# Scores and value products of both row tiles issued as one group in every attention

## The chip, the cores and the metric

One NeuronCore of a Trainium2 chip runs the kernel. The metric is the device time of one execution in microseconds (us). The engines are named as the profile names them: PE is TensorE (PEld its weight loads), DVE is VectorE, ACT is ScalarE, POOL is GpSimd, SP the engine that issues the DMAs.

## The reference, cut to what matters

Two decoder layers over 256 positions of width 1024, all in float32. Each layer projects the normed input and runs four causal mixers of 4 heads x 64; one of them, NSA, has three parts, of which two are ordinary attentions here. So a layer has five attentions of the same form (DSA with a mask of selected keys, MoBA, two of NSA, and SWA with a sink and a band of 128):

```
h = rms_norm(x, norm1_g[l]);  proj = h @ w_in[l]
ya = dsa_mixer(...); yb = moba_mixer(...); yc = nsa_mixer(...); yd = swa_mixer(...)
br = einsum('bsnc,ncd->bsnd', [ya, yb, yc, yd], w_branch[l])
x = x + einsum('bsnd,bsnd->bsd', sigmoid(g_br), br) @ w_out[l]
x = x + conv_ffn(rms_norm(x, norm2_g[l]), ...)

each attention:  s = q k^T * scale;  p = masked_softmax(s, ok, sink);  o = p v
NSA:             g0 * o_compressed + g1 * o_selected + g2 * o_window
```

## The kernel before, in words

The 256 positions are two row tiles of 128 (`NT` = 2); row tile t sees 128 (t + 1) keys. Every large product takes its float32 operands as a rounded high part and a low part (`hi`, `lo`; fp32r), three matmuls for each. ACT makes the high part of the weights and DVE the low part, in pieces of 128 x 1024, just ahead of their use.

The order on each engine is written by a planner in the kernel itself (`Flow`, line 86). Every part of the work is a Python generator, a stream. It asks for an engine, the times that it needs and the buffers that it wants (`yield "PE", needs, rings`), and then issues instructions. `Flow.run` (line 139) goes on each time with the stream that can start first by its own estimate of durations (`Eng.cost`, line 180); of equal starts the lower priority number goes first. A request for several buffers waits until all are free. The chip then runs each engine's instructions in that fixed order.

`main` (line 1261) is the stream that fills PE. For each layer it issues the projections, then gates, hidden products and branches in the order of `SEQ` (line 398): gate 0 twice, hidden 0 and 1, gate 1 twice, branch 0 and 1 (two halves each), gate 2 twice, branch 2 (two halves), gate 3, branch 3, gate 3, branch 3. A gate takes 48 matmuls of 512 columns into two banks. A branch half takes 12 and needs the finished result `yf` of its mixer, split by `y_T` (line 587). `hidden` (line 1039) needs `hid.ready`, from the first part of `nsa`.

There are eight PSUM banks in three rings: `mm_r` with four, `sc_r` with two, `tr_r` with two (lines 252 to 254). `main` takes its banks from `mm_r`, two at a time (first branch halves from `sc_r` once all mixers are done).

`attend(t, ...)` (line 642) is one attention for one row tile; each attention spawns two such streams, with neighbouring priorities. It takes a softmax buffer `sx_r` (a ring of two), small columns `sm_r` (four) and both banks of `sc_r`. Its scores are four matmuls on row halves of the array (64 rows contract; even and odd heads lie in the two halves and write different banks). Then `attend_max` (line 747) reads the banks on DVE with scale, mask and running maximum; after that come exponentials on ACT, the reciprocal, the scaling, transposes of the probabilities on PE through `tr_r`, their copy into a buffer of `pt_r` (a ring of two), and the value products on column halves of the array (64 output rows each). The result is copied, or for NSA added, into `y`. In the trace a score matmul is `sc<-qk` with 64*128 in front, a value product `tr<-f,slotQ` or `tr<-f,kvA` with 128*64; a float32 matmul leaves two records, so a score group has 8 records, and a value group has 8 for row tile 0 and 16 for row tile 1.

`nsa` needs its compressed part `y0` before its two attentions begin. The hidden products also use small tiles (128*15).

## Time and profile before

| | us |
|---|---|
| median of three runs (849.93 to 850.3) | 850.2 |
| the profiled execution | 850.6 |
| its span, first to last instruction | 848.8 |
| PE busy | 839.5 (99%) |
| DVE busy | 668.4 (79%) |
| ACT busy | 549.6 (65%) |

A view of the timeline gives start and duration in us, the engine, the line (every instruction is recorded at the helper's line 215), the operation, what it writes and reads, and its shape; "x8" is a run of eight instructions merged into one row, and in brackets stands idle time of the engine in front of it. PE's matmuls are pipelined, so a duration is longer than the distance between starts; it is the starts that give the pace.

### The profile page before, as it was taken

How to read it: one execution, taken by the hardware profiler on the slowest of the kernel's cores; microseconds unless marked ns; L12 is line 12 of the kernel's file. 1: busy time of each engine (PE TensorE's matmuls, PEld its weight loads, DVE VectorE, ACT ScalarE, POOL GpSimd, SP SyncE). 2: the span in 40 equal slices, each digit the busy share in tenths (PEclk: the TensorE clock that was granted, in tenths of full speed). 3: DMA queues.
4: the chain of work that ended last, by engine and by line, in shares of the span. 5: the costliest groups of instructions: out<-in, count | busy, mean ns of one | idle time of the engine just before them, and what ended most of it. 6: DMA issues, size and time to landing. Idle time of an engine off the chain costs nothing.

```text
span 848.8 us, 14195 instructions
## 1 busy us (share of the span) xinstructions
PE 839.5 (99%) x5457; PEld 730.2 (86%) x5457; DVE 668.4 (79%) x1310; ACT 549.6 (65%) x968; POOL 34.2 (4%) x33
## 2 busy tenths in 40 slices
PE   9999999999999999999999999999999999999998
PEld 8987777778889999988899877777788999999886
DVE  5899897867669999985457998898856799999552
ACT  6664965664558888864356568567645788888431
POOL 0011111000000000000001010110000000000000
PEclk9999999999999999999999999999999999999999
DMA  7754444525646665546445564544365465556550
GB/s 264 248 199 149 147 164 150 182 80 203 217 151 205 212 206 196 188 151 219 146 131 179 195 198 158 191 149 143 110 200 193 149 199 198 200 198 199 176 196 26
DMA packets 103415, 149.92 MB, mean 177 GB/s; under 512 B 4072, under 2 KB 62258, under 8 KB 103346
## 3 DMA queue, kind: packets, MB, share of 16 engines
q1 hardware_dynamic: 103346, 149.00, 52.5%
q8 instruction: 43, 0.70, 0.4%
q14 instruction: 26, 0.21, 0.1%
HBM read 147.94 MB, written 1.05 MB: 176 GB/s over the span
## 4 chain that ended last, share of the span: by engine, by line
PE 85%; DVE 8%; DMA 3%; ACT 2%; issue 1%; POOL 0%; SPq 0%; DVEq 0%; ACTq 0%
PE mm L215 74%; PE tr L215 6%; PE sc L215 5%; DVE lo L215 2%; DMA raw<-in_w_in_dram 2%; DVE acc L215 2%; DVE m L215 1%; ACT f L215 1%; DVE f L215 1%; DMA x<-in_x_dram 1%; ACT hi L215 1%; DVE rt L215 0%; SPq L243 0%; POOL rkC L215 0%; DVE kr L215 0%
## 5 line engine op out<-in xcount | busy, mean ns | idle before, releaser
L215 DVE TENSOR_TENSOR lo<-raw,hi 128x1024 fp32r<-128x1024 f32 (+2 forms) x280 | 328.4, 1177 | 103.2 <-ACT hi L215 99.2
L215 ACT ACTIVATE hi<-raw 128x1024 fp32r<-128x1024 f32 (+2 forms) x280 | 283.5, 1022 | 147.8 <-PE mm L215 131.0
L215 PE MATMUL mm<-hi,ahi 128*128 128x512 f32 (+4 forms) x480 | 176.2, 373 | 0.6 <-ACT hi L215 0.6
L215 PE MATMUL mm<-hi,alo 128*128 128x512 f32 (+4 forms) x480 | 171.9, 364 | 0.4 <-DVE alo L215 0.4
L215 PE MATMUL mm<-ahi,hi 128*128 128x256 f32 x640 | 149.8, 276 | 0.0
L215 PE MATMUL mm<-alo,hi 128*128 128x256 f32 x640 | 149.6, 276 | 0.0
L215 PEld LDWEIGHTS mm<-alo,hi 128*128 128x128 f32 x640 | 120.2, 188 | 0.1
L215 PEld LDWEIGHTS mm<-ahi,hi 128*128 128x128 f32 x640 | 120.1, 188 | 0.1
L215 PE MATMUL mm<-lo,ahi 128*128 128x512 f32 (+4 forms) x480 | 119.0, 371 | 0.0
L215 PEld LDWEIGHTS mm<-hi,ahi 128*128 128x128 f32 x480 | 90.2, 188 | 14.1 <-issue 1.1
L215 PEld LDWEIGHTS mm<-hi,alo 128*128 128x128 f32 x480 | 90.4, 188 | 12.6 <-DVE alo L215 0.7
L215 PEld LDWEIGHTS mm<-lo,ahi 128*128 128x128 f32 x480 | 82.6, 188 | 14.6 <-issue 2.9
L215 PE MATMUL mm<-hi,slotQ 128*128 128x512 f32 x352 | 89.7, 395 | 0.0
L215 PE MATMUL mm<-ahi,lo 128*128 128x256 f32 x640 | 86.9, 276 | 0.0
L215 PEld LDWEIGHTS mm<-hi,slotQ 128*128 128x128 f32 x352 | 66.1, 188 | 15.5
L215 PEld LDWEIGHTS mm<-ahi,lo 128*128 128x128 f32 x640 | 79.1, 188 | 0.0
L215 ACT ACTIVATE f<-f,col 128x256 f32<-128x256 f32 x88 | 48.1, 594 | 6.3 <-DVE f L215 5.8
L215 PE MATMUL mm<-lo,slotQ 128*128 128x512 f32 x176 | 48.7, 396 | 0.0
L215 ACT ACTIVATE f<-f,nmx 128x128 f32<-128x128 f32 (+1 forms) x80 | 35.5, 446 | 13.1 <-DVE nmx L215 13.1
L215 PEld LDWEIGHTS mm<-lo,slotQ 128*128 128x128 f32 x176 | 33.0, 188 | 7.7
L215 ACT ACTIVATE qk<-f,col 128x256 f32<-128x256 f32 x88 | 39.2, 495 | 0.0
L215 DVE SCALAR_TENSOR_TENSOR f<-f,col,f 128x254 f32<-128x254 f32 x88 | 38.2, 477 | 0.0
(229 smaller groups left out, 1037.8 us busy)
## 6 DMA issues: line engine op xcount, KB each, us to landing
raw<-in_w_up_dram SPq DMA_DIRECT2D x44, 1024.0 KB, 5.1
raw<-in_w_in_dram SPq DMA_DIRECT2D x40, 1024.0 KB, 4.9
raw<-in_w_down_dram SPq DMA_DIRECT2D x20, 1024.0 KB, 4.9
raw<-in_w_out_dram SPq DMA_DIRECT2D x8, 1024.0 KB, 4.9
raw<-in_w_branch_dram SPq DMA_DIRECT2D x6, 1024.0 KB, 4.8
raw<-in_w_in_dram SPq DMA_DIRECT2D x7, 768.0 KB
raw<-in_w_in_dram SPq DMA_DIRECT2D x4, 592.0 KB, 3.7
raw<-in_w_in_dram SPq DMA_DIRECT2D x4, 536.0 KB, 5.6
```

The costliest lines, as they stand in the source:

```text
L215: fn(*a, **k)
```

## The change

`attend` is replaced by three streams. `attend2` asks once for two softmax buffers, two sets of small columns, two banks of `mm_r` (row tile 0) and two of `sc_r` (row tile 1), and issues the scores of both row tiles, eight matmuls, in one group. `softmax` runs once for each row tile with what stood between scores and value products, and `values` waits for all transposed probabilities of both row tiles, issues the 12 value matmuls in one group into one bank of `tr_r`, and makes one copy or addition of the whole `y`. `SEQ` and `main` stay as they are. The planner's cost of a matmul changes as well: it charged 95 when the type of operand changed between fp32 and fp32r, and now charges 100 when the tile shape (`side`) does.

```diff
@@ -175,7 +175,7 @@
 
     def __init__(self, flow, name, real):
         self.flow, self.name, self.real = flow, name, real
-        self.side, self.rounded = 1, True
+        self.side, self.tiled = 1, 1
 
     def cost(self, m, a, k):
         aps = [v for v in list(a) + list(k.values()) if hasattr(v, "shape")]
@@ -186,10 +186,9 @@
             if m == "transpose":
                 c = 0.835 * n
             else:
-                r = a[1].dtype == F32R
-                c = 0.446 * n + 2 if r else 1.67 * max(n, free_size(a[1])) + 2
-                if r != self.rounded:
-                    c, self.rounded = c + 95 * self.side, r
+                c = 0.446 * n + 2 if a[1].dtype == F32R else 1.67 * max(n, free_size(a[1])) + 2
+                if self.side != self.tiled:
+                    c, self.tiled = c + 100 * self.side, self.side
             return c / self.side * (1 if self.flow.clock["PE"] > 6700 else 2)
         ptrs = sum(hasattr(k.get(q), "shape") for q in ("scale", "bias", "accum_out", "scalar"))
         if self.name == "ACT":
@@ -639,23 +638,56 @@
         tr_r.give(tb, te)
         return te
 
-    def attend(t, qT, kblk, kT, vfn, scl, mask, y, needs, sink=None, fin=None, gate=None):
+    def attend2(prio, qT, kblk, kT, vfn, scl, masks, y, needs, sink=None, fin=None, gates=None):
+
+        got = yield "PE", needs, [sx_r, sm_r, sx_r, sm_r, mm_r, mm_r, sc_r, sc_r]
+        P.side = 2
+        for t in range(NT):
+            nk = 128 * (t + 1)
+
+            for hh in range(2):
+                for par in range(2):
+                    b = 64 * par
+                    te = P.matmul(got[4 + 2 * t + par][:, hh * nk:hh * nk + nk], qT[b:b + 64, hh, t * 128:t * 128 + 128],
+                                  kT[b:b + 64, kblk(2 * hh + par), :nk], start=True, stop=True)
+        P.side = 1
+        pts, evs = [None, None], [[Fut() for _ in range(t + 1)] for t in range(NT)]
+        for t in range(NT):
+            fl.spawn(softmax(t, got[2 * t], got[2 * t + 1], got[4 + 2 * t:6 + 2 * t], (mm_r, sc_r)[t], te, scl, masks[t], sink,
+                             None if gates is None else gates[t], pts, evs[t]), prio + t)
+        yield from values(vfn, pts, evs, y, gates is not None, fin)
+
+    def values(vfn, pts, evs, y, more, fin):
+
+        ob, = yield "PE", evs[0] + evs[1], [tr_r]
+        op = ob.rearrange("p (k q) -> p k q", k=2)
+        P.side = 2
+        for t in range(NT):
+            pT = pts[t].rearrange("p (h b q) -> p h b q", h=H, b=2)
+            for k in range(2):
+                for b in range(t + 1):
+                    for par in range(2):
+                        te = P.matmul(op[64 * par:64 * par + 64, k, t * 128:t * 128 + 128], vfn(2 * k + par, b),
+                                      pT[:, 2 * k + par, b, :], start=b == 0, stop=b == t)
+            pt_r.give(pts[t], te)
+        P.side = 1
+        if not more:
+            eng, _ = yield "AV", [te], []
+            te = copy_on(eng, y, op)
+        else:
+            yield "DVE", [te], []
+            te = V.tensor_tensor(y, y, op, op=ALU.add)
+        tr_r.give(ob, te)
+        fin(te)
+
+    def softmax(t, sxt, sm, scs, ring_, te, scl, mask, sink, gate, pts, tes):
         nk = 128 * (t + 1)
         rdf = Fut()
         tx = []
-        sxt, sm, *scs = yield "PE", needs, [sx_r, sm_r, sc_r, sc_r]
         Sx = sxt.rearrange("p (h n) -> p h n", h=H)
         mx, nmx, den, es, rd = (sm[k] for k in ("mx", "nmx", "den", "es", "rd"))
-
-        P.side = 2
-        for hh in range(2):
-            for par in range(2):
-                b = 64 * par
-                te = P.matmul(scs[par][:, hh * nk:hh * nk + nk], qT[b:b + 64, hh, t * 128:t * 128 + 128],
-                              kT[b:b + 64, kblk(2 * hh + par), :nk], start=True, stop=True)
-        P.side = 1
         for par in range(2):
-            fl.spawn(attend_max(t, scs[par], te, par, Sx, nk, mask, scl, sink, mx, tx), 8)
+            fl.spawn(attend_max(t, scs[par], te, par, Sx, nk, mask, scl, sink, mx, tx, ring_), 8)
         yield "DVE", [_Pair(tx)], []
         tm = V.tensor_scalar(nmx, mx, -1.0, None, op0=ALU.mult)
         for h in range(H):
@@ -678,11 +710,10 @@
                 tn.append(A.activation(Sx[:, h, :nk], Sx[:, h, :nk], AF.Copy, scale=rd[:, h:h + 1]))
             else:
                 tn.append(V.tensor_scalar(Sx[:, h, :nk], Sx[:, h, :nk], rd[:, h:h + 1], None, op0=ALU.mult))
-        tes = []
-        pTt = None
         for g in range(t + 1):
             if g == 0:
                 pTt, tb = yield "PE", tn if t == 0 else tn[:2], [pt_r, tr_r]
+                pts[t] = pTt
                 pT = pTt.rearrange("p (h b q) -> p h b q", h=H, b=2)
             else:
                 tb, = yield "PE", tn[2:], [tr_r]
@@ -697,31 +728,9 @@
                     for b in range(2):
                         tq = P.transpose(tp[:, hh, b, :], Sx[:, 2 * g + hh, b * 128:b * 128 + 128], ident)
                 dst = pT[:, 2 * g:2 * g + 2]
-            f = Fut()
-            tes.append(f)
-            fl.spawn(evac_tr(dst, tp, tb, tq, f), 9)
+            fl.spawn(evac_tr(dst, tp, tb, tq, tes[g]), 9)
         sx_r.give(sxt, tq)
         sm_r.give(sm, max(tn))
-
-        ob, = yield "PE", tes, [tr_r]
-        op = ob[:, :256].rearrange("p (k q) -> p k q", k=2)
-        P.side = 2
-        for k in range(2):
-            for b in range(t + 1):
-                for par in range(2):
-                    te = P.matmul(op[64 * par:64 * par + 64, k, :], vfn(2 * k + par, b), pT[:, 2 * k + par, b, :],
-                                  start=b == 0, stop=b == t)
-        P.side = 1
-        pt_r.give(pTt, te)
-        yt = y[:, :, t * 128:t * 128 + 128]
-        if gate is None:
-            eng, _ = yield "AV", [te], []
-            te = copy_on(eng, yt, op)
-        else:
-            yield "DVE", [te], []
-            te = V.tensor_tensor(yt, yt, op, op=ALU.add)
-        tr_r.give(ob, te)
-        fin(te)
 
     def recip(t2, den, rd, gate, f):
         yield "DVE", [t2], []
@@ -744,14 +753,14 @@
         def t(self):
             return max(self.l) if len(self.l) == 2 else None
 
-    def attend_max(t, sc, te, par, Sx, nk, mask, scl, sink, mx, tx):
+    def attend_max(t, sc, te, par, Sx, nk, mask, scl, sink, mx, tx, ring_):
         for hh in range(2):
             h = 2 * hh + par
             yield "DVE", [te], []
             td = V.tensor_tensor_reduce(Sx[:, h, :nk], sc[:, hh * nk:hh * nk + nk], mask, scale=scl[:, t, h:h + 1],
                                         scalar=LOW if sink is None else sink[:, h:h + 1],
                                         op0=ALU.add, op1=ALU.max, accum_out=mx[:, h:h + 1])
-        sc_r.give(sc, td)
+        ring_.give(sc, td)
         tx.append(td)
 
     def evac_tr(dst, tp, tb, te, f):
@@ -844,10 +853,9 @@
         tq = yield from T_pairs(qT, qr, 2, [tq])
         tk = yield from T_pairs(kT, krd, 1, [tk])
         prep_r.give(prep, tk)
-        fin = qk_done(qk, [], yf, NT)
-        for t in range(NT):
-            fl.spawn(attend(t, qT, lambda h: 0, kT, lambda h, b: kvA[:, b, 64:128], th(sm1["sA"], H), sel[t],
-                            y, [tq, tk, self_f[t]], fin=fin), 10 + t)
+        fin = qk_done(qk, [], yf, 1)
+        fl.spawn(attend2(10, qT, lambda h: 0, kT, lambda h, b: kvA[:, b, 64:128], th(sm1["sA"], H), sel,
+                        y, [tq, tk] + self_f, fin=fin), 10)
 
     def indexer(t, iqT, ikT, iw, needs, fin, f):
         nk = 128 * (t + 1)
@@ -901,10 +909,9 @@
         tk = yield from rope(kr.rearrange("p t (h u d) -> p t h u d", u=1, d=64), heads(kn), H, DH, cc[:, 3], ss_[:, 3], rt, [tn])
         tk = yield from T_pairs(kT, kr, 2, [tk])
         prep_r.give(prep, tk)
-        fin = qk_done(qk, [], yf, NT)
-        for t in range(NT):
-            fl.spawn(attend(t, qT, lambda h: h // 2, kT, lambda h, b: pb[:, b, 512 + 64 * h:576 + 64 * h],
-                            th(sm1["sB"], H), tri[:, 128 * (1 - t):], y, [tq, tk], fin=fin), 20 + t)
+        fin = qk_done(qk, [], yf, 1)
+        fl.spawn(attend2(20, qT, lambda h: h // 2, kT, lambda h, b: pb[:, b, 512 + 64 * h:576 + 64 * h],
+                        th(sm1["sB"], H), [tri[:, 128:], tri], y, [tq, tk], fin=fin), 20)
 
     def swa(l, pd, pf, y, yf):
         (prep,) = yield "ACT", [pf, tab_f[l]], [prep_r]
@@ -923,11 +930,10 @@
         tk = yield from rope(kr.rearrange("p t (h u d) -> p t h u d", h=2, d=64), knv, 2, DH, cc[:, 9], ss_[:, 9], rt, [tn], dup=2)
         tk = yield from T_pairs(kT, kr, 2, [tk])
         prep_r.give(prep, tk)
-        fin = qk_done(qk, [], yf, NT)
-        for t in range(NT):
-            fl.spawn(attend(t, qT, lambda h: h // 2, kT,
-                            lambda h, b: pd[:, b, 384 + 64 * (h // 2):448 + 64 * (h // 2)], th(sm1["sD"], H),
-                            tri[:, 128:] if t == 0 else dmask, y, [tq, tk], sink=M[l]["sink"], fin=fin), 30 + t)
+        fin = qk_done(qk, [], yf, 1)
+        fl.spawn(attend2(30, qT, lambda h: h // 2, kT,
+                        lambda h, b: pd[:, b, 384 + 64 * (h // 2):448 + 64 * (h // 2)], th(sm1["sD"], H),
+                        [tri[:, 128:], dmask], y, [tq, tk], sink=M[l]["sink"], fin=fin), 30)
 
     def nsa(l, pc, pf, y, yf, hid):
         m = M[l]
@@ -1010,7 +1016,7 @@
         tr_r.give(tb, te)
         y0 = [Fut(), Fut()]
         fl.spawn(nsa_cmp(qT, [te, tq], tvb, cgv, y, y0), 12)
-        fin = qk_done(qk, [], yf, 2 * NT)
+        fin = qk_done(qk, [], yf, 2)
         last = list(y0)
         for i, g in ((0, 6), (1, 7)):
             off = 384 + 128 * i
@@ -1025,10 +1031,9 @@
             tk = yield from T_pairs(kTi, krd, 1, [tk])
             if i == 1:
                 prep_r.give(prep, tk)
-            for t in range(NT):
-                fl.spawn(attend(t, qT, lambda h: 0, kTi, lambda h, b, off=off: pc[:, b, off + 64:off + 128],
-                                th(sm1["sC"], H), tri[:, 128 * (1 - t):], y, [tq, tk, y0[t]],
-                                fin=fin, gate=cgv[:, t, :, 1 + i]), 13 + 2 * i + t)
+            fl.spawn(attend2(13 + 2 * i, qT, lambda h: 0, kTi, lambda h, b, off=off: pc[:, b, off + 64:off + 128],
+                             th(sm1["sC"], H), [tri[:, 128:], tri], y, [tq, tk, y0[0]],
+                             fin=fin, gates=[cgv[:, t, :, 1 + i] for t in range(NT)]), 13 + 2 * i)
 
     class Hidden:
 
```

## Rows read from the trace of the kernel before

**Rows 1.** The page: busy us, share of the span and instructions of each engine.

```profile
PE 839.5 (99%) x5457; PEld 730.2 (86%) x5457; DVE 668.4 (79%) x1310; ACT 549.6 (65%) x968; POOL 34.2 (4%) x33
```

**Rows 2.** Windows: stretch, its us, busy us of each engine (instructions), PEclk, DMA share, GB/s.

```profile
56.00:109.50 53.50, 52.56 (x319) 40.75 (x317) 51.28 (x161) 39.26 (x87) 5.17 (x2) 1.00 0.42 138
109.50:187.20 77.70, 76.44 (x478) 59.49 (x477) 62.57 (x175) 47.77 (x114) 6.03 (x3) 1.00 0.45 156
...
451.00:610.00 159.00, 157.99 (x989) 126.75 (x989) 140.11 (x391) 107.52 (x229) 12.96 (x8) 1.00 0.48 163
```

**Rows 3.** Timeline of PE around a score group of row tile 0.

```profile
89.09 0.40 PE L215 MATMUL mm<-hi,alo 128*128 128x512 f32 x1
89.42 0.72 PE L215 MATMUL sc<-qk 64*128 64x128 f32 x8
90.06 0.50 PE L215 MATMUL mm<-hi,ahi 128*128 128x512 f32 x1
90.40 0.39 PE L215 MATMUL mm<-hi,alo 128*128 128x512 f32 x1
```

**Rows 4.** Timeline of PE, a value group directly followed by a score group, row tile 1.

```profile
95.31 0.40 PE L215 MATMUL mm<-hi,alo 128*128 128x512 f32 x1
95.64 1.09 PE L215 MATMUL tr<-f,kvA 128*64 128x128 f32 x16
96.66 1.14 PE L215 MATMUL sc<-qk 64*128 64x256 f32 x8
97.72 0.74 PE L215 MATMUL mm<-lo,ahi 128*128 128x512 f32 x2
```

**Rows 5.** Timeline of PE, a full-size fp32 group and matmuls behind it.

```profile
33.38 0.61 PE L215 MATMUL tr<-kvup,kn 128*128 128x128 f32 x4
...
33.95 0.29 PE L215 MATMUL mm<-hi,alo 128*128 128x268 f32 x1
34.07 0.29 PE L215 MATMUL mm<-hi,ahi 128*128 128x268 f32 x1
```

**Rows 6.** Timeline of PE, last gate matmuls and the hidden products, layer 0.

```profile
102.54 0.86 PE L215 MATMUL mm<-lo,ahi 128*128 128x512 f32 x3
...
109.53 1.94 PE L215 MATMUL mm<-raw,kr 128*15 128x128 f32 x64
```

**Rows 7.** Timeline of DVE: merge, first mask-and-max step, and the split behind the fourth.

```profile
146.23 1.28 DVE L215 SCALAR_TENSOR_TENSOR mg<-mg,mm 128x512 f32<-128x512 f32 x2
147.43 0.34 DVE L215 CUSTOM_DVE_ANT_0 f<-sc,cst,sC 128x128 f32<-128x128 f32 x1
...
148.51 1.22 DVE L215 TENSOR_TENSOR lo<-raw,hi 128x1024 fp32r<-128x1024 f32 x1
```

**Rows 8.** Timeline of PE, score groups of NSA, and last that of SWA.

```profile
146.35 0.71 PE L215 MATMUL sc<-qk 64*128 64x128 f32 x8
...
165.02 0.71 PE L215 MATMUL sc<-qk 64*128 64x128 f32 x8
...
168.80 1.14 PE L215 MATMUL sc<-qk 64*128 64x256 f32 x8
...
571.56 0.72 PE L215 MATMUL sc<-qk 64*128 64x128 f32 x8
...
578.80 1.13 PE L215 MATMUL sc<-qk 64*128 64x256 f32 x8
...
594.35 1.13 PE L215 MATMUL sc<-qk 64*128 64x256 f32 x8
```

**Rows 9.** Timeline of DVE, low part of the result of branch 2, both layers.

```profile
183.66 0.69 DVE L215 TENSOR_TENSOR ylo<-slotQ,yhi 128x512 fp32r<-128x512 f32 x1 [0.70 <-ACT yhi L215]
...
598.92 0.68 DVE L215 TENSOR_TENSOR ylo<-slotQ,yhi 128x512 fp32r<-128x512 f32 x1
```

**Rows 10.** Timeline of PE, first matmul of branch 2, both layers.

```profile
187.13 0.39 PE L215 MATMUL sc<-hi,yhi 128*128 128x512 f32 x1
...
602.34 0.40 PE L215 MATMUL mm<-hi,yhi 128*128 128x512 f32 x1
```

## Prediction

> **What bounds the kernel now.** I read the page's busy table first. TensorE works 839.5 of 848.8 us [rows 1], so a term counts only if it takes time from TensorE's queue, or makes that queue wait. The windows by stage come second [rows 2]. Attention lies in three of them: layer 0 before and after its hidden products (56 to 109.5 and 109.5 to 187.2) and layer 1 (451 to 610). TensorE is idle for 0.94, 1.26 and 1.01 us there, at a granted clock of 1.00; VectorE is busy 51.28 of 53.50 us in the first, 62.57 of 77.70 in the second, 140.11 of 159.00 in the third. So TensorE sets the time nearly everywhere, and VectorE is close behind it in the first stage.
>
> The timeline of TensorE, third, shows what the small attention matmuls cost. Plain matmuls of 512 columns start every 0.23 us. Around a score group of row tile 0 the starts are 89.09, 89.42, 90.06, 90.40 [rows 3]: from the start of the last matmul ahead to that of the second matmul behind there are 1.31 us, of which 2 x 0.23 are the ordinary pace, so the group costs 0.85. Its content comes from the next group: a score group of row tile 1 has four steps of 256 columns in place of 128 and takes 97.72 - 96.66 = 1.06, against 90.06 - 89.42 = 0.64 [rows 3, 4]; the difference, 0.42, is the price of four steps of 128 columns. So the isolated group holds 0.42 of work and 0.43 of something else, about half at its entry and half at its exit.
>
> Value products have the same thing. A value group of row tile 1 (eight steps of 128 columns, 0.84) followed directly by a score group (0.84) takes from 95.31 to 97.72, 2.41, less 0.23 for the matmul ahead, plus 0.11 by which the first matmul behind a group is late (90.40 - 90.06 - 0.23) [rows 3, 4]: 2.29 - 1.68 = 0.61 for three changes: full array to column halves, column halves to row halves, row halves to full. Both give 0.2 us for one change. Is it the tile shape or the type? A group of four full-size fp32 records begins at 33.38, and the second matmul behind it at 33.95; the next, at 34.07, shows the pace of those 268 columns, 0.12 [rows 5]. 33.95 - 33.38 - 0.12 = 0.45 for four, 0.11 each, as a step of the score group has without its changes: nothing is left for a change. So the tile shape is what costs, and fewer blocks of small tiles mean less TensorE time.
>
> **The change part by part.** *Blocks.* Each layer has five attentions with two score and two value groups each, 40 groups in all: 80 changes. In the trace ten pairs of a score and a value group stand directly behind each other (the first from 95.64 [rows 4], the last from 594.35 [rows 8]), and each saves one; one more is shared with the hidden products [rows 6]. So there are 69: 17 before 109.5, 18 to 187.2, 34 in layer 1. Afterwards there are 20 groups and at most 40 changes. Since the next scores become possible with the last transposes of the pair before, and its values only after their copy, some will again stand side by side; there are 8 places where one attention follows another, and I take 4, with 0 and 8 as ends. 69 - 36 = 33 changes x 0.2 = 6.6 us, between 5.8 (29) and 7.4 (37). By stage: 8, 9 and 16, that is 1.6, 1.8 and 3.2 us. The columns multiplied stay the same.
>
> *What of it counts.* In layer 0 the main stream has nothing from 102.54 + 0.86 to the hidden products at 109.53 [rows 6]: those wait for a chain of VectorE, which is saturated. TensorE time saved ahead of that point only lengthens this wait, unless the chain gets shorter. I count the 1.6 there at nothing (ends 0 and 1.6). 1.8 + 3.2 = 5.0 us remain.
>
> *Banks.* Scores of row tile 0 move from the ring of two to the ring of four that the main stream uses two at a time. They are held until the mask-and-max steps have read them. The nearest row: the group at 146.35 is read until 148.51, 2.2 us [rows 7, 8]; with row tile 1's 0.84 in front of the reading, 3.0. In layer 0's first NSA attention this meets the branch products: two banks are being merged (146.23 + 1.28) and two are filling. The pair can start at 147.5 and takes 0.42 + 0.84 + 0.43 = 1.7, to 149.2; its first four readings (1.08 from 147.43 to 148.51) then end at 150.3, or with one split of 1.22 ahead of them at 151.5 [rows 7]. The branch that is filling ends 12 x 0.23 + 1.7 behind 146.35, at 150.8, and the next one wants these banks: 0 to 0.7, I take 0.4. For the other nine: the main stream changes banks every 48 x 0.23 = 11 us, so 9 x 3.0/11 = 2.5 holds cover a change. A wait lasts at most what is left of the hold, on the mean 1.5, so 0 to 3.7 in all; other attention work fills some, and I take 1.4.
>
> *Waits that are added.* The pair needs both selection masks, both softmax buffers and both transposed tiles. DSA's row tile 0 now waits for row tile 1's mask too. No one waits for its result: the merge of that branch stands only at 146.23 in layer 0 [rows 7]. What queues behind it on VectorE is moved but not grown. The only attention with a near reader is the second NSA one. Its result is ready for the branch at 183.66 + 0.69 = 184.35 and 598.92 + 0.68 = 599.60 [rows 9], and the branches start at 187.13 and 602.34 [rows 10]: 2.8 and 2.7 us of cover. In its favour, the first NSA pair's row tile 1 no longer waits for the two score banks of row tile 0. I set what pairing does to this chain at nothing, and price its failure below. Joining two result copies saves ACT or VectorE some tenths beside TensorE: nothing. The planner's new price charges an isolated group as before within 10 ns, so it gives no reason for another order beyond the groups themselves.
>
> Sum: 5.0 - 0.4 - 1.4 = 3.2 us. The profiled execution took 850.6 (span 848.8): 847.4. The median of the runs is 850.2, 0.4 lower: **847.0**.
>
> **The rivals.** *The whole saving comes through.* The hidden products move forward too, because row tile 0's DSA work no longer stands in front of the selection chain, and the bank waits vanish: 6.6 to 7.4, about 843. For it: VectorE's total is unchanged. Against it: the chain also runs through single buffers and GpSimd.
>
> *Banks eat it.* All bank waits at their upper ends: 0.7 + 3.7 = 4.4 of 5.0, so 849.6, about 850. The sign would be main-stream matmuls idle behind a mask-and-max. Against it: most holds last 2 to 3 us of 11. The Trainium skill, TensorEngine Tiling (Array Packing), Performance Considerations (PSUM Bottleneck), says that tiling speeds up TensorE but not the emptying of PSUM, which may then set the pace. By that rule the time is this rival's 850; reading 128 columns takes 0.27 us (1.08 / 4) against 0.1 on TensorE (0.42 / 4), which agrees with it, while TensorE's idle time of about 1 us a stage does not yet show it as the limit.
>
> *Pairing delays the last NSA chain: slower.* In layer 1 the two row tiles of the second NSA attention start at 571.56 and 578.80 [rows 8], 7.2 us apart, because row tile 0 takes the first softmax buffer that comes free. Paired, both start with the later. If row tile 0's work can't go beside row tile 1's, the result comes up to 7.2 later. The cover is 2.7, and the gates end earlier but the branch can't: 7.2 - 2.7 = 4.5 over the old time, whatever was saved ahead; layer 0 adds at most 1 (its starts are 165.02 and 168.80, 3.8 apart, against 2.8). That is 850.8 to 856; with three quarters of the lead lost, 7.2 x 0.75 - 2.7 = 2.7, about 853. It decides from a delay of 2.7 us on. Against it: both engines that run the softmax have gaps in that stretch (VectorE 140 of 159 [rows 2]), and the first pair ends earlier.
>
> That the change doesn't do what it says is not open: one request takes four banks and issues both row tiles.
>
> **How the numbers follow.** Forecast (845 to 849): 0.45. Whole saving: 0.18. Banks eat it: 0.17. Slower: 0.20. A measurement of this kernel tells about 0.2% (1.7 us) from no change, so faster 0.63, same 0.17, slower 0.20. The range runs from 842.5 to 853: it leaves out the best end of the saving (0.06) and the upper end of the slower case (0.1).
>
> **What would show it.** TensorE's busy time should fall by about 6 us, at the same number of matmul records, with 16 records in a score block and 24 in a value block. Its idle time in the middle should grow by about 3, of which 1.6 before the hidden products of layer 0. Branch 2's first matmul should stand directly behind a gate. I am wrong if TensorE sits idle ahead of that branch (third rival), if it sits idle ahead of plain gate matmuls with the releaser VectorE (second), or if the blocks cost as much as two.

## The result and the profile after

The changed kernel takes 860.06 us (median of four runs, 859.14 to 861.45) against 850.07 of the kernel before on the same chip: ratio 1.0122, 95% interval 1.0110 to 1.0134. It is slower by 10 us where 3 us of gain were forecast, and it lies above the range. The profiled execution took 859.14 us. Its page begins:

```profile
span 857.4 us, 14193 instructions
...
PE 838.2 (98%) x5459; PEld 734.6 (86%) x5459; DVE 670.9 (78%) x1315; ACT 546.8 (64%) x953; POOL 35.7 (4%) x33
```

Against [rows 1] TensorE works 1.3 us less, in a span that is 8.6 us longer. So the loss is waiting of TensorE, and work at a lower clock. It shows in the windows of [rows 2] (columns as there):

```profile
56.00:109.50 53.50, 47.89 (x277) 38.98 (x276) 50.90 (x158) 35.26 (x77) 6.08 (x2) 0.98 0.42 138
109.50:187.20 77.70, 76.77 (x510) 61.51 (x509) 64.27 (x184) 49.41 (x114) 4.79 (x3) 0.97 0.43 150
...
451.00:610.00 159.00, 152.76 (x957) 124.85 (x956) 136.70 (x384) 101.16 (x212) 15.80 (x9) 1.00 0.49 164
```

TensorE now idles 5.61 us in the first window (0.94 before) and 6.24 in the third (1.01), and the granted clock, 1.00 in all of them before, is 0.98 and 0.97 in the first two. The timeline of TensorE shows the first place (answering [rows 3, 4, 6]; the count of the last row is cut by the end of the view):

```profile
97.66 0.72 PE L214 MATMUL mm<-qk 64*128 64x128 f32 x8
98.20 1.03 PE L214 MATMUL sc<-qk 64*128 64x256 f32 x8
99.17 1.53 PE L214 MATMUL tr<-f,kvA 128*64 128x128 f32 x24
100.63 1.19 PE L214 MATMUL mm<-lo,ahi 128*128 128x512 f32 x4
101.66 0.60 PE L214 MATMUL tr<-cst,qr 128*128 128x128 f32 x4
105.71 0.63 PE L214 MATMUL tr<-cst,kr 128*128 128x128 f32 x4 [3.45 <-DVE den L214]
...
108.63 1.12 PE L214 MATMUL tr<-cst,f 128*128 128x128 f32 x4 [1.47 <-DVE f L214]
...
112.04 1.23 PE L214 MATMUL mm<-qk 64*128 64x128 f32 x8
113.05 1.70 PE L214 MATMUL sc<-qk 64*128 64x256 f32 x8
114.68 1.53 PE L214 MATMUL tr<-f,slotQ 128*64 128x128 f32 x24
116.14 1.29 PE L214 MATMUL mm<-raw,kr 128*15 128x128 f32 x40
```

The joined blocks are as designed: 1.51 us for 16 score records, 1.46 for 24 value records. But TensorE has run out of work at about 102.3. It waits 3.45 us ahead of the transposes of SWA's keys, then 1.47, and the hidden products start at 116.14 instead of 109.53. Windows around the pause (columns as above):

```profile
101.80:107.50 5.70, 1.85 (x13) 1.10 (x10) 5.63 (x26) 5.58 (x21) 0.00 (x0) 1.00 0.47 175
107.50:114.50 7.00, 5.48 (x28) 4.33 (x28) 6.90 (x17) 4.44 (x10) 0.00 (x0) 0.51 0.00 0
114.50:117.00 2.50, 2.50 (x60) 2.15 (x60) 1.93 (x11) 0.71 (x2) 0.00 (x0) 1.00 0.53 151
```

After a stretch with 1.85 us of work in 5.70 the granted clock is 0.51, that is the lower level, 1.2 GHz. The score block that took 1.51 us at full clock takes 2.64 (112.04 to 114.68). The second place is branch 2 of layer 1, on TensorE and on VectorE (answering [rows 9, 10]; `yhi` and `ylo` are the high and low part of the mixer's result, `slotQ<-slotQ,tr` is the addition of a value product):

```profile
601.01 1.53 PE L214 MATMUL tr<-f,slotQ 128*64 128x128 f32 x24
...
607.16 0.50 PE L214 MATMUL mm<-hi,yhi 128*128 128x512 f32 x1 [2.58 <-ACT yhi L214]
608.50 0.50 PE L214 MATMUL mm<-hi,ylo 128*128 128x512 f32 x1 [0.84 <-DVE ylo L214]
```

```profile
601.43 0.41 DVE L214 CUSTOM_DVE_ANT_0 f<-mm,cst,sink 128x128 f32<-128x128 f32 x1
...
604.15 0.54 DVE L214 CUSTOM_DVE_ANT_0 f<-sc,cst,sink 128x256 f32<-128x256 f32 x1
...
604.62 0.69 DVE L214 TENSOR_TENSOR slotQ<-slotQ,tr 128x512 f32<-128x512 f32 x1
...
607.76 0.68 DVE L214 TENSOR_TENSOR ylo<-slotQ,yhi 128x512 fp32r<-128x512 f32 x1
```

The last NSA value block is issued at 601.01 and takes 1.46, but its addition starts at 604.62. On VectorE it stands behind the eight mask-and-max steps of SWA, 601.43 to 604.62, which before came in two lots of four; the addition then stood behind one lot:

```profile
595.41 1.09 PE L215 MATMUL tr<-f,slotQ 128*64 128x128 f32 x16
```

```profile
595.52 0.55 DVE L215 CUSTOM_DVE_ANT_0 f<-sc,cst,sink 128x256 f32<-128x256 f32 x1 [1.44 <-PE sc L215]
...
597.38 0.42 DVE L215 TENSOR_TENSOR slotQ<-slotQ,tr 128x256 f32<-128x256 f32 x1
```

Branch 2 waits 2.58 + 0.84 us, and the clock is then at half for 3.4 us. The view of TensorE's waits has the same items at its head (total us, times, longest):

```profile
PE tr L214 <- DVE den L214: 3.4, 1, 3.4
PE mm L214 <- ACT yhi L214: 2.6, 1, 2.6
PE tr L214 <- DVE f L214: 1.9, 2, 1.5
...
PE mm L214 <- DVE slotP L214: 1.5, 1, 1.5
```

### The profile page after: what moved, and what is told of

Same layout as the page of the kernel before. It is cut to its first block, busy times and chain, and to the rows that moved or that the text cites. A ratio compares the mean times of both kernels' runs of the same rounds, so it can differ in the third digit from the quotient of the medians.

```text
span 857.4 us, 14193 instructions
## 1 busy us (share of the span) xinstructions
PE 838.2 (98%) x5459; PEld 734.6 (86%) x5459; DVE 670.9 (78%) x1315; ACT 546.8 (64%) x953; POOL 35.7 (4%) x33
## 4 chain that ended last, share of the span: by engine, by line
PE 83%; DVE 9%; ACT 2%; DMA 2%; POOL 2%; issue 1%; SPq 0%; DVEq 0%; ACTq 0%
PE mm L214 72%; PE tr L214 6%; PE sc L214 5%; DVE lo L214 2%; DVE acc L214 2%; DMA raw<-in_w_in_dram 1%; ACT f L214 1%; DVE m L214 1%; DVE rt L214 1%; POOL rB L214 1%; DVE f L214 1%; DMA x<-in_x_dram 1%; ACT hi L214 1%; POOL rqA L214 0%; DVE qr L214 0%
```

## The experiments

Below, "at 8" and "at 25" is the planner's priority of the mask-and-max steps (the readings of the score banks). "Layer 1 begins" is the start of its first matmul on `kvup` in the trace; "layer 1" is what follows, to the end of the span. Ratios and intervals are against the kernel before on the same chip, whose medians lie between 849.70 and 850.09. e7 and e10 have the planner's price of the kernel before, all others the new one; so what the request or the joining costs is read from pairs with the same price.

| run | readings | softmax buffers | joined | us | ratio (95%) | layer 1 begins | layer 1 |
|---|---|---|---|---|---|---|---|
| before | 8 | own | none | 850.07 | | 451.2 | 397.7 |
| after | 8 | both at once | both | 860.06 | 1.0110-1.0134 | 454.7 | 402.7 |
| e1 | 8 | own | none | 851.48 | 1.0014-1.0033 | 453.3 | 396.1 |
| e2 | 8 | own | values | 854.44 | 1.0041-1.0071 | 456.8 | 395.4 |
| e3 | 8 | both at once | scores | 859.87 | 1.0106-1.0140 | 455.4 | 403.0 |
| e5 | 8 | both at once | none | 858.42 | 1.0090-1.0121 | 458.1 | 398.3 |
| e6 | 8, NSA first | both at once | both | 887.68 | 1.0436-1.0492 | 454.0 | 431.0 |
| e7 | 8, NSA first | own | none | 872.58 | 1.0244-1.0288 | 448.2 | 421.6 |
| e8 | 8, NSA first | own | values | 874.71 | 1.0268-1.0313 | 446.1 | 423.6 |
| e9 | 25 | both at once | both | 849.56 | 0.9987-1.0007 | 450.6 | 398.7 |
| e10 | 25 | own | none | 847.05 | 0.9954-0.9977 | 448.4 | 396.8 |
| e11 | 25 | own | values | 845.31 | 0.9931-0.9960 | 447.3 | 395.5 |
| e12 | 25 in layer 0 | both at once | both | 855.37 | 1.0057-1.0091 | 448.6 | 402.8 |
| e13 | 25 in layer 1 | both at once | both | 853.30 | 1.0026-1.0060 | 454.9 | 396.6 |
| e15 | 25 | both at once | none | 851.28 | 1.0009-1.0028 | 449.9 | 399.1 |
| e16 | 25 | both at once | scores | 850.16 | 0.9991-1.0011 | 448.2 | 400.3 |
| e17 | 25 | own | both | 842.93 | 0.9906-0.9936 | 446.2 | 394.9 |
| e18 | 8 | own | both | 851.18 | 1.0009-1.0028 | 453.6 | 396.8 |
| e19 | 8, NSA's chain first | both at once | both | 853.40 | 1.0022-1.0051 | 454.8 | 396.8 |
| e20 | as its attention | own | both | 852.54 | 1.0020-1.0045 | 454.7 | 396.0 |

### The parts of the change, one at a time

e1: the kernel before with only the new planner price.

```diff
-                if r != self.rounded:
-                    c, self.rounded = c + 95 * self.side, r
+                if self.side != self.tiled:
+                    c, self.tiled = c + 100 * self.side, self.side
```

> The kernel before with the planner's new matmul price alone, no group joined. Request theory (the joint request for softmax buffers, banks and both masks delays the attention chains) and values theory (the joint value group waits for the slower row tile): both expect 850, within 1.5 us, with the hidden products of layer 0 near 109.5 us. Planner theory (the new price alone moved the order): 855 or more, hidden products of layer 0 near 116 us.

Measured 0.24% more, some 2 us: nearer to the first two theories' 850, while the hidden products, at 112.45, lie midway. The price alone reorders both layers: layer 0 is 2.1 us longer, layer 1 1.5 shorter. It is not the cause of the 10 us, but in layer 0, where the changed kernel loses 3.5 us, it is no small thing.

e2: value products joined, scores as before, each row tile with its own request.

```diff
+        sxt, sm, *scs = yield "PE", needs, [sx_r, sm_r, sc_r, sc_r]
...
+        ob, = yield "PE", evs[0] + evs[1], [tr_r]
```

> Of the change, only the value products are joined; scores are requested per row tile, as before, from the two banks of the score ring. Request theory: 846 to 850, since the ten value groups saved give about 2 to 4 us of TensorE and the chains stay. Values theory: 856 to 860, with the second NSA result of layer 1 late for its branch.

Measured 4.5 us more, outside both ranges. All of it lies in layer 0 (5.7); layer 1 is 2.3 shorter, so the second NSA result isn't late. There is idle time on TensorE ahead of SWA's keys here too.

e3: scores joined, value products per row tile.

```diff
+        got = yield "PE", needs, [sx_r, sm_r, sx_r, sm_r, mm_r, mm_r, sc_r, sc_r]
...
+        for t in range(NT):
+            fl.spawn(values(t, vfn, pts, evs[t], y, gates is not None, fin), prio + t)
```

> Of the change, only the scores are joined; each row tile has its own value group. Request theory: 856 to 861, idle TensorE ahead of the hidden products of layer 0 as in the changed kernel. Values theory: 846 to 850.

Measured the whole loss of the changed kernel, as the request theory has it: 859.87.

e5: nothing joined; only the request is.

```diff
+        got = yield "PE", needs, [sx_r, sm_r, sx_r, sm_r]
...
+        scs = yield "PE", needs, [sc_r, sc_r]
```

> No group is joined, but both softmax buffers, both sets of columns and both masks are asked for at once, as the changed kernel does; the scores then take the two score banks one row tile after the other. Request theory: 858 to 864 (the delay of the changed kernel, without what joining saves on TensorE). If what costs is the burst of eight mask-and-max steps behind one joint score group, or its banks: 850 to 854.

Measured 858.42, inside the request theory's range: most of the loss is there without any joined matmul and without the projections' banks. Against e1, which differs in the joint request (buffers, columns, masks) alone, it is 6.9 us. But it lies elsewhere: 4.8 us in layer 0 and 2.2 in layer 1 (398.3). The changed kernel and e3, where scores are joined as well, lose most in layer 1 (402.7 and 403.0).

### Which attention gets the single prologue buffer first

MoBA, NSA and SWA share one buffer for their prologue (norm, rotation and transposes ahead of the scores). In layer 0, in before and after, SWA gets it ahead of NSA, on which the hidden products hang. e6 to e8 let NSA ask on another engine, which puts it first: the changed kernel (e6), the kernel before (e7), and the one with values joined (e8).

```diff
-        (prep,) = yield "DVE", [pf, tab_f[l]], [prep_r]
+        (prep,) = yield "ACT", [pf, tab_f[l]], [prep_r]
```

> The changed kernel, with one word changed: NSA asks for the prologue's single working buffer as the other mixers do, so that in layer 0 it gets it ahead of SWA, as it does in layer 1 already. Theory H (layer 0 loses because the chain to its hidden products, which has SWA's prologue and the attention work in front of it, has no slack): hidden products of layer 0 at or before 106 us instead of 116, no half clock there, and 853 to 856 for the kernel; what is left is layer 1's. Theory P (what costs in layer 0 is the joint request wherever the hidden products stand): 858 to 861.

> The kernel before with the same word changed. Both theories: hidden products of layer 0 some us earlier than 109.5; 847 to 850, since at most the idle time and the stand of the main stream ahead of them can go (0.8 and 0.8 us idle there).

> Value products joined, scores separate (as e2), with the same word changed. Theory H: the 7 us that e2 lost ahead of the hidden products of layer 0 come back and what joined values save on TensorE stays (16 changes of 0.2 us): 845 to 848, under the kernel before. Theory P: 852 to 855, as e2.

As totals all three missed widely. The table says where: layer 1, which the word also reorders, becomes 24 to 28 us longer. Layer 0 by itself did what the idea says: the hidden products start at 102.4, 102.0 and 101.9, and layer 1 begins 3.0 us earlier than in the kernel before (e7), 10.8 earlier than with values joined (e8), but only 0.7 earlier with the joint request (e6). TensorE in e6 shows why, in layer 0 (the first row's count is cut by the end of the view):

```profile
102.37 0.85 PE L214 MATMUL mm<-raw,kr 128*15 128x128 f32 x24 [0.55 <-ACT mg L214]
...
184.10 0.51 PE L214 MATMUL mm<-hi,yhi 128*128 128x512 f32 x1 [2.58 <-ACT yhi L214]
185.44 0.50 PE L214 MATMUL mm<-hi,ylo 128*128 128x512 f32 x1 [0.83 <-DVE ylo L214]
```

Branch 2 now waits in layer 0 just as it does in layer 1, by the same 2.58 us. Why layer 1 becomes so long in these three was not followed further.

### The readings of the score banks

e9: the changed kernel, with the mask-and-max steps behind the other steps of VectorE when both could start.

```diff
-            fl.spawn(attend_max(t, scs[par], te, par, Sx, nk, mask, scl, sink, mx, tx, ring_), 8)
+            fl.spawn(attend_max(t, scs[par], te, par, Sx, nk, mask, scl, sink, mx, tx, ring_), 25)
```

> The changed kernel, the mask-and-max steps spawned at priority 25 instead of 8, behind the small steps and the NSA additions. Theory B (in layer 1 branch 2 waits because eight readings of the next attention's joint scores stand ahead of the addition of the second NSA result on VectorE): the wait of 3.4 us ahead of branch 2 shrinks to under 1.5 and the half clock behind it goes, 855 to 858. If the wait comes from the chain's own lateness: 859 to 862.

849.56: the whole loss of 10 us is gone, more than expected, though TensorE still idles in both layers. e10 and e11 have the same number in the kernel before and in the one with values joined.

> The kernel before, with nothing joined, and with one number changed: its mask-and-max steps stand at priority 25 in the planner instead of 8. Theory B (the fault of the change is that eight of these steps come free at one moment and are put ahead of everything else on VectorE): here only four come free at a time, as they always did, so the priority has little to give, 848 to 852 us. Theory P (late reading is good for any version of this kernel, and the joining has no part in it): the gain that the changed kernel had from it, 10 us, appears here too, about 840 us. A third reading (any number in the planner throws the order about by some microseconds): anywhere between 845 and 858, with layer 0 and layer 1 moving in no common direction.

> Value products of both row tiles in one group, scores per row tile as in the kernel before, and the mask-and-max steps at priority 25. With priority 8 this was 854.4 us. Theory B: its bursts are the old ones of four, so little of its 4.4 us loss lies in the reading order, 851 to 855 us. Theory P: ten us less, about 844, which would beat both kernels.

Neither theory is right as stated. The kernel before gains 3.0 us, a little more than theory B gave and far from the 10 of theory P. Values joined gains 9.1, about what P gave, where B gave at most 3.4, though its readings come in fours as before. So a burst of eight isn't needed for the loss of layer 0. What all runs with 25 in layer 0 have in common is the order that e6 to e8 forced, as their traces show: NSA's prologue ahead of SWA's. Their hidden products start at 100.7 to 102.5 (seven runs); with 8, or with the attention's own priority, and NSA not forced first, at 109.5 to 117.0 (ten kernels, before and after among them). Late reading and forced order give layer 0 nearly the same length where buffers are requested singly: 448.4 and 448.2 with nothing joined, 447.3 and 446.1 with values joined.

e12 and e13 set 25 in one layer only.

```diff
+    ..., ring_), 25 if fl.clock["PE"] < 300000.0 else 8)     # e12: layer 0
+    ..., ring_), 8 if fl.clock["PE"] < 300000.0 else 25)     # e13: layer 1
```

> The changed kernel with its mask-and-max steps at priority 25 in layer 0 and at 8 in layer 1. Layer 0 should be that of the kernel with the late reading throughout (layer 1 starts at about 450.6 us instead of 454.7), and layer 1 should keep its wait of some 3.4 us before branch 2. Theory B (each layer loses by its own burst, and the losses add): 860.1 - 4.1 = 856 us, 854.5 to 857.5. If the loss is one event whose effect carries over from layer 0, the whole gain appears here: about 850.

> The changed kernel with its mask-and-max steps at priority 25 in layer 1 alone. Layer 0 is that of the changed kernel, with the idle time and the half clock of TensorE near 102 to 114 us. Theory B: layer 1 takes 4 us less (398.7 instead of 402.7 us, as in the kernel with the late reading throughout), so 856 us, 854.5 to 857.5, and the two gains of this run and of the one with layer 0 alone add up to about 10 (4.1 + 4 shown by the milestones, the rest open). If layer 0 alone carries the loss: 859 to 861.

855.37 and 853.30, the second a little better than expected: 4.7 and 6.8 us, together 11.5 against the 10.5 of e9. The losses of the two layers are separate and roughly add up. In the traces layer 0 of e12 gains 6.1 us and layer 1 of e13 6.0; in e9's trace, which has 3.4 us at half clock in each layer, they gain 4.1 and 4.0.

e19: readings left at 8; only NSA's two attentions go ahead of them.

```diff
-                             fin=fin, gates=[cgv[:, t, :, 1 + i] for t in range(NT)]), 13 + 2 * i)
+                             fin=fin, gates=[cgv[:, t, :, 1 + i] for t in range(NT)]), 5 + i)
```

> The changed kernel with the readings left at priority 8 and the request left joint; only the two last attentions of NSA stand at 5 and 6 instead of 13 and 15, so that their own softmax steps and the additions of their value products go ahead of the readings of SWA on VectorE. If the loss of late layer 1 is that the last NSA addition stands behind SWA's eight readings (branch 2 waits 2.6 + 0.8 us, and the clock is then at half for 3.4 us): these waits go, and the time is 853 to 857 us, layer 0 unchanged. If the loss lies in the readings of the same attention standing ahead of its other row tile's steps (a burst of its own eight readings), nothing changes in the time, 858 to 862 us, and the distance of the last two value blocks of NSA stays at about 16 us.

853.40, inside the first theory's range, with layer 0 unchanged (454.8) and layer 1 5.9 us shorter. VectorE and TensorE at the place of the loss:

```profile
599.63 0.69 DVE L214 TENSOR_TENSOR slotQ<-slotQ,tr 128x512 f32<-128x512 f32 x1 [1.00 <-PE tr L214]
600.24 0.54 DVE L214 CUSTOM_DVE_ANT_0 f<-sc,cst,sink 128x256 f32<-128x256 f32 x1
...
601.17 0.69 DVE L214 TENSOR_TENSOR ylo<-slotQ,yhi 128x512 fp32r<-128x512 f32 x1
```

```profile
602.30 1.08 PE L214 MATMUL mm<-lo,ahi 128*128 128x512 f32 x4
603.22 0.40 PE L214 MATMUL mm<-hi,yhi 128*128 128x512 f32 x1
```

The addition no longer stands behind the last four readings, and branch 2 follows its gate with no wait. Layer 1 is back at its old length, so its loss comes from what goes ahead of NSA's last chain on VectorE. It isn't the addition alone: the edit moves all steps of that chain, and its value block, too, comes 3.1 us earlier in the layer.

### The joint request for both softmax buffers

With late reading, joined values still gain (e11), but joined scores cost: e9 is 4.3 us above e11. e15 and e16 are e5 and e3 at 25; e17 and e18 keep all joined groups and undo only the request, e17 at 25, e18 at 8.

```diff
-        got = yield "PE", needs, [sx_r, sm_r, sx_r, sm_r, mm_r, mm_r, sc_r, sc_r]
+        got = yield "PE", needs, [mm_r, mm_r, sc_r, sc_r]
...
+        sxt, sm = yield "DVE", [te], [sx_r, sm_r]     # in softmax, per row tile
```

> Nothing joined in the groups; both softmax buffers and both column sets of an attention requested at once, as in the earlier run with the joint request, and the mask-and-max steps at priority 25. With 25 throughout, the kernel before took 847.05 us, value products joined 845.3, both joined 849.6. Theory S (what is left of the loss is that an attention must hold both softmax buffers before its first score, so that two attentions no longer overlap: the value blocks of the two last NSA attentions in layer 1 lie 11.4 us apart with values joined and 13.6 with both joined): about 13.6 us apart here too, and with the tile-shape changes not saved, 852 to 856 us. Theory K (the loss is that the four score banks are held together, two of them those of the projections): the request costs little, 846 to 849 us.

> Scores of both row tiles in one group with four banks, value products apart, mask-and-max steps at priority 25. Theory S and theory K both expect a time above that with nothing joined (847.05): S because it contains the joint request, 850 to 854, and about as long as the run with the request alone less the 18 saved changes of tile shape (3 us); K expects the whole loss here and none in the run with the request alone. If this run is at 844 to 847, joined scores are harmless and it is joining both that costs.

> The changed kernel (scores joined with four banks, values joined), mask-and-max steps at 25, and each row tile's softmax requests its own buffer and columns after the score group, instead of both ahead of it. Theory S: the value blocks of the last two NSA attentions come back to 11.4 to 12.5 us apart, and the time to 842 to 846 us (845.3 of values joined less 18 changes of about 0.18 us, that is 842, up to no gain). Theory K: the banks are held as long or longer, since the reader of a bank now waits for its buffer, 850 to 854 us.

> The changed kernel with its own priorities (8) and only the buffer request undone: each row tile's softmax requests its own buffer after the score group. Theory S alone would put some 4 us back (860.1 to about 856), since the readings still stand ahead of the chains' other steps, which was worth 10. If reading order is the lasting cause and the buffers matter only beside it, 857 to 860. Theory K: 860 to 864.

Theory S holds, with other sizes. e15 takes 851.28, between the two ranges, with its value blocks 14.5 us apart where S gave 13.6; e16 (850.16) and e17 lie in S's ranges. In the pairs that differ in nothing else, the request for the softmax buffers costs 6.6 us at 25 (e9 against e17) and 8.9 at 8 (the changed kernel against e18). (e15 against e10 gives 4.2, but there the price differs too.) Without it the four banks cost nothing at 25: e17 takes 842.93, the fastest of all and 0.8% below the kernel before. e18 does better than S gave: 8.9 us of the 10 come back with the readings still at 8. In the traces, which differ by 7.0, 5.9 lie in layer 1 (396.8) and 1.1 in layer 0, which at 453.6 is about where the price alone puts it (e1). The attention blocks of layer 1 in e17, on TensorE:

```profile
572.68 0.71 PE L214 MATMUL mm<-qk 64*128 64x128 f32 x8
573.23 1.03 PE L214 MATMUL sc<-qk 64*128 64x256 f32 x8
580.24 1.53 PE L214 MATMUL tr<-f,slotQ 128*64 128x128 f32 x24
581.70 0.71 PE L214 MATMUL mm<-qk 64*128 64x128 f32 x8
...
589.28 1.53 PE L214 MATMUL tr<-f,slotQ 128*64 128x128 f32 x24
593.63 0.39 PE L214 MATMUL mm<-hi,yhi 128*128 128x512 f32 x1
```

and in e9, which differs in the request alone:

```profile
582.76 1.53 PE L214 MATMUL tr<-f,slotQ 128*64 128x128 f32 x24
594.93 0.71 PE L214 MATMUL mm<-qk 64*128 64x128 f32 x8
595.48 1.03 PE L214 MATMUL sc<-qk 64*128 64x256 f32 x8
596.44 1.53 PE L214 MATMUL tr<-f,slotQ 128*64 128x128 f32 x24
599.42 0.50 PE L214 MATMUL mm<-hi,yhi 128*128 128x512 f32 x1 [1.45 <-ACT yhi L214]
```

Between the last two value blocks of NSA lie 9.0 us in e17, 13.7 in e9 and 15.9 in the changed kernel (585.10 to 601.01). In the kernel before it was 15.6 (579.86 to 595.41), so this distance by itself isn't what made the change slower. With both buffers in one request, an attention can't start before the one ahead of it has released both: the next score block comes only after both row tiles' transposes (594.93 in e9). With own requests it needs only its banks: in e17 both score blocks are issued ahead of the last transposes of the attention before (at 577.42 and 586.47).

e20: own requests, and the readings at the priority of their attention.

```diff
-            fl.spawn(attend_max(t, scs[par], te, par, Sx, nk, mask, scl, sink, mx, tx, ring_), 8)
+            fl.spawn(attend_max(t, scs[par], te, par, Sx, nk, mask, scl, sink, mx, tx, ring_), prio)
```

> Each row tile's softmax requests its own buffer, and the mask-and-max steps take the priority of their own attention (10, 13, 15, 20, 30) instead of 25 for all, so that NSA's readings come ahead of MoBA's and SWA's, and those of all still behind divisions and evacuations (8 and 9). With 25 this took 842.9 us, with 8 it took 851.2. If what counts is that readings stand behind the divisions and evacuations of every chain, 841 to 845 us; if it also counts that they stand behind the softmax steps and additions of the other attentions, it falls between, 845 to 850.

852.54, above both ranges. Layer 1 is fine (396.0), and layer 0 is as long as in the changed kernel (454.7), but not for the same reason throughout. The hidden products start at 111.4, 4.7 us earlier. Later TensorE waits 1.60 us for a bank of the projections' ring (to 158.66), while an NSA pair, issued at 154.13, holds two of that ring until its readings end at 162.9; and it is then at half clock for 3.4 us. So the banks can cost where their readings come late. By their priorities the readings of DSA and MoBA, at 10 and 20, still pass the prologues of NSA or SWA (19 and 21), and SWA's prologue still goes first; that this is why was not tested.

## Why the prediction was wrong

*The blocks: right, a little too large.* The trace counts 70 changes of tile shape before and 34 after, 36 saved where 33 were forecast. TensorE's busy time at full clock (half of the 8.8 us that it worked at half clock taken off) falls from 839.5 to 838.2 - 4.4 = 833.8: 5.7 us, 0.16 a change instead of 0.2. Between e10 and e17, where little waits, it is 5.0 for 33, 0.15 each. Single pairs of kernels scatter: the six with nothing joined lie between 837.6 and 840.6 (mean 839.4), the nine with both joined between 832.7 and 836.0 (mean 833.9), 5.4 apart. That bare saving is what joining is worth; 4.1 us reach the time between e10 and e17 (the price differs there too).

*The banks: the number by luck.* 0.4 + 1.4 us were set down. The trace has one wait for a bank, 1.47 us at gate 2 of layer 1, to 572.86, with VectorE as the releaser, the second rival's sign. But no score group holds a bank of that ring then (its last readings end at 564.6). What TensorE waits for is the merge of branch 1 (`slotP`), behind other work on VectorE. The second rival, four banks as the limit, didn't come about: e17 takes the same four and is the fastest run. By the rule cited with it (the Trainium skill, TensorEngine Tiling (Array Packing), Performance Considerations, PSUM Bottleneck) emptying the banks could have set the pace; in e17, where TensorE waits 0.2 us for a bank in all, it doesn't, while e20 has a wait of 1.60 us of that kind.

*The hidden products of layer 0: the first step that failed.* The prediction saw that TensorE has nothing to do ahead of them and that they hang on a saturated VectorE, and wrote that saved time is lost there "unless the chain gets shorter". It priced no longer chain. They start 6.6 us later (109.53 to 116.14). SWA's prologue goes ahead of NSA's through the one buffer, as before, but now all eight readings of MoBA stand directly ahead of SWA's keys (`kn`), where before four of them had come nine us ahead of it: the scores of MoBA's row tile 0 are issued at 97.66 instead of 89.42, as the pair has to wait for both softmax buffers. On VectorE before, with the last step ahead of the hidden products (`kr<-kn,col`):

```profile
90.34 0.34 DVE L215 CUSTOM_DVE_ANT_0 f<-sc,cst,sB 128x128 f32<-128x128 f32 x1
...
100.47 0.42 DVE L215 TENSOR_TENSOR kn<-slotQ,rD 128x256 f32<-128x256 f32 x1
...
109.00 1.18 DVE L215 TENSOR_TENSOR kr<-kn,col 128x120 f32<-128x120 f32 x4
```

and in the changed kernel:

```profile
100.24 0.34 DVE L214 CUSTOM_DVE_ANT_0 f<-mm,cst,sB 128x128 f32<-128x128 f32 x1
...
103.14 0.48 DVE L214 CUSTOM_DVE_ANT_0 f<-sc,cst,sB 128x256 f32<-128x256 f32 x1
...
103.62 0.42 DVE L214 TENSOR_TENSOR kn<-slotQ,rD 128x256 f32<-128x256 f32 x1
...
112.27 1.15 DVE L214 TENSOR_TENSOR kr<-kn,col 128x120 f32<-128x120 f32 x4
```

"What queues behind it on VectorE is moved but not grown" is the sentence at fault. The work is the same, but moved ahead of the chain that the hidden products wait for: SWA's keys come 3.2 us later and the chain's last step 3.3. The other 3.3 us are on TensorE: the joined blocks of SWA's scores and MoBA's values, 112.04 to 116.14, for 2.4 us of it at half clock, go ahead of the hidden products, which before started 0.53 us behind that step and now 3.87. That the hidden products hang on which prologue goes first is shown by e6 to e8. That the readings' place is enough to undo the loss of the layer is shown by e12; how the 3.5 us of layer 0 split is not, since the price alone gives 2.1 (e1) and without the joint request 2.4 stay (e18).

*The planner's price: a step set at nothing.* "It gives no reason for another order" doesn't hold: with the price alone the time is 0.14 to 0.33% longer, and the order in layer 0 another one (e1).

*Pairing: the second step, and the third rival's place.* "I set what pairing does to this chain at nothing" was wrong. Counted from the start of layer 1, the low part of branch 2's result comes 5.3 us later (598.92 - 451.16 against 607.76 - 454.70), where the cover was 2.7. The rival named the chain, the cover and the sign (TensorE idle ahead of that branch, as the prediction's last part has it), and gave 853; but it put the delay down to the pair's own row tiles. Of the 5.3 us, 2.1 lie ahead of the last value block (595.41 - 451.16 against 601.01 - 454.70), which alone would stay within the cover. Another 1.6 lie between the block and its addition, behind eight readings of SWA instead of four, and 1.6 behind the addition, where ACT makes `yhi` 1.2 us after the addition's end. e13 and e19 show that the place of SWA's readings against NSA's chain makes the loss of this layer, and e18 that it goes without the joint request for the softmax buffers; e5 shows that the request alone isn't enough here, the joined scores are needed too. The prediction listed that request among the waits. It asked who needs DSA's mask and when the NSA pair can start, but not what the request does to the order of the other attentions.

*The clock: no term at all.* The two pauses were followed by 6.8 and 3.4 us at half clock, in which TensorE worked 8.8 us: 4.4 us lost. The account by the profiles: -5.7 for the blocks, +9.8 idle time on TensorE (9.3 to 19.1), +4.4 for the clock gives +8.5, and the span grew by 8.6. This divides TensorE's time; it doesn't say what the time would be at full clock. In layer 0 of e13 and e19, with the same order, the half clock lasted 10.2 us instead of 6.8, and the hidden products started at 116.30 and 116.25, hardly later than 116.14.

*The range.* Its upper end took one late chain, most of it in one layer. Chains were late in both; reading later gives back 4.7 us in one and 6.8 in the other (e12, e13).

## What to carry to other kernels

Where one stream takes at one moment what two took before, ask not only what the joined work costs but what else becomes ready with it, and look at the priorities by which it is queued: here eight short readings on VectorE went ahead of the chains that TensorE was waiting for. Request what is needed at different times in different requests: two softmax buffers asked for together stopped neighbouring attentions from overlapping, at 7 to 9 us. Joining both groups gained only once both were mended (842.93 against 849.75 on the same chip), and a cover of 3 us on an engine at 90% is to be priced both ways.

## What of the hardware was not expected

A pause of TensorE can cost more than itself. After 1.85 us of work in 5.70 the granted clock was 0.51 for some 7 us, and after the 2.58 and 0.84 us of waiting at branch 2 it was at half for 3.4 us, with TensorE at work all the time. The kernel before, with waits of at most 1 us in these stages, was at 1.00 throughout.

The same pauses don't always cost it. Layer 0 of e9 and of e12 is the same program, and near 175 to 182 us TensorE pauses for 1.5, 1.65 and 0.38 us in both traces. In e9 the clock was then at half for 3.4 us, in e12 it stayed at 1.00; layer 1 begins at 450.6 and 448.6.

A change of tile shape costs 0.15 to 0.16 us in the whole kernel, where single isolated groups showed 0.2.
